# Twelve of sixteen gate channel tiles from half-depth block products, ahead of the attention heads

## The chip, the cores and the metric

The kernel runs on one core of a Trainium2 chip. The metric is the device time of one execution in microseconds. The profile's times count from the start of its own span, which is a little shorter than the device time of a run.

## What is computed

One layer of a block that joins a convolution branch and an attention branch, on 1024 tokens of 1024 channels, in float32. Cut to what matters here:

```python
h = rms_norm(x, norm1_g)
glu_in, q, k, v, gate_logits = split(h @ w_in)       # gate_logits: 2 x 1024 channels
a = glu(glu_in); a = depthwise_conv(a, conv_w) + conv_b
y_a = silu(rms_norm(a, conv_norm_g)) @ w_conv_out
o = dilated_window_attention(rms_norm(q), rms_norm(k), v)     # 16 heads of 64
y_b = o @ w_attn_out
g_a, g_b = split(sigmoid(gate_logits + gate_b))
x = x + (g_a * y_a + g_b * y_b) @ w_out
x = x + glu(conv3(rms_norm(x, norm2_g) @ w_up)) @ w_down
```

The change concerns `gate_logits`: 2048 gate channels by 1024 tokens, each a sum over 1024 channels of the normed x.

## The kernel before

Every float32 operand of a matrix product is split into a high part (a rounded copy, made on ScalarE) and a low part (the rest, a subtraction on VectorE), and each product is made of three TensorE matmuls: high x high, high x low, low x high (`split` L77, `gemm_half` L106). A plain gate tile of 128 channels by 512 tokens over the full depth of 1024 is thus 8 steps of 3 matmuls of 128x128 by 512.

The stages are, in order: norm1, its transposed high and low parts `hT`, and the GLU with first products (to about 181 us); the q, k, v products (loop at L607, to 457 us), with the convolution on VectorE and ScalarE beside them and a little beyond; the sixteen heads (to about 902 us); the merge with w_attn_out and w_out; the up projection, convolution of width 3 and the down projection, both of which already work by seven half-depth products instead of eight (`product` L971).

The gates and `w_conv_out` have no stage of their own. `side_steps` (L179) is a generator that gives out one step (three matmuls) at a time: 32 uses of gate weights (16 channel tiles, two token halves, L198 `gate`) and 16 of `w_conv_out` (L215 `conv_out`), 8 steps each, 384 in all. Per use it stages the weights by a 512 KB DMA, and asks for their splits as pieces of 128x512, which are handed out one by one (`piece_high` on ScalarE, `piece_low` on VectorE). The gate's sum leaves PSUM by a ScalarE activation that adds the bias (L210), and is stored to DRAM (`dgate`); the merge loads it again and takes the sigmoid (L834, L835).

Who asks for steps: `cover` (L641) takes 15, 8 and 20 steps around the end of the convolution branch and its norm (L650 to L676). Then the heads: 128 slots (16 heads, two halves of 512 queries, four blocks of 128 each). In each slot PE does the score of one block (`score`, two matmuls for each stretch of keys), the transposes of an earlier block (`flip`, BACK = 5 slots behind) and its product with v (`weigh`, L731 and L732); VectorE takes the masked minimum (L702), ScalarE the exponential (L707), GpSimd the division (L711); ScalarE and VectorE split the transposed block (L79, L80). Between these, `fill` (L749) takes steps from `side_steps`, by the rates in FILL, whose sum over eight slots is 17.5. What is left of the steps is done behind the last slot.

In the heads the program's order on ScalarE, VectorE and TensorE is kept as written (`tc.manual_schedule`); elsewhere a scheduler orders each engine's instructions at build. DMAs are issued by SyncE in one order (some by ScalarE); a DMA waits there for the one eight places ahead, and for what its data and its buffer need, and all behind it wait too. The loads of head 0 (`head(0)`, L625: six of 256 KB for q, kh, kl and one of 512 KB for the mask m) are issued before the gates begin, into a pool of their own (`p2i`), and those of head h + 1 in the third slot of head h.

Behind the heads, the merge (L825) takes, for each of eight output tiles and two halves, 24 matmuls `yb` of w_attn_out with the heads' output `oT`, which is loaded back from DRAM and split.

Of the kernel before, what the change touches and what calls it, by code (L numbers as in the profile page):

```python
# [13 lines left out]
F32 = mybir.dt.float32  # L14
# [21 lines left out]
FILL = (1.5, 3.4, 1.8, 1.9, 1.6, 3.0, 2.1, 2.2)  # L36
BACK = 5
SHARE = 0.6
COVER = (15, 8, 20)
# [14 lines left out]
def block_kernel(ctx: ExitStack, tc: tile.TileContext, x, xT, x0, g2, pack, mask,  # L54
# [76 lines left out]

    def spill(dst, src):
        sp.dma_start(dst.bitcast(F32), src.bitcast(F32))
# [7 lines left out]
    dv = [dr.tile([P, 8, 8, P], F32R, name=f"dv{i}") for i in range(2)]  # L141
    dgate = [dr.tile([P, T], F32, name=f"dgate{i}") for i in range(16)]
# [36 lines left out]
    def side_steps(hT, da):  # L179
# [18 lines left out]
        def gate(c, half):  # L198
            def go(w):
                gp = bank_ps(f"gate_{c}_{half}")  # L200
                if c >= 12 and half == 1:
                    if not aT:
                        aT.extend(hb_tiles(hb1, "aT"))
                    ask_conv(0, 2 * (c - 12))
# [5 lines left out]
                act.activation(sg, gp, AF.Identity, bias=pk[:, C_GB + c : C_GB + c + 1])  # L210
# [19 lines left out]
        for c in range(12):  # L230
            for half in range(2):
                gate(c, half)
        for half in range(2):
            for c in range(12, 16):
                gate(c, half)
        for c0 in (0, 4):
# [8 lines left out]
        for i, (_, n, go) in enumerate(uses):  # L245
# [7 lines left out]
            if n.startswith("co"):  # L253
                need = max(need, marks[(i - 32) // 4 % 2])
# [25 lines left out]
    with tc.tile_pool(name="ph1", bufs=1) as p1:  # L280
# [157 lines left out]
        with tc.manual_schedule(engines={ENG.Activation, ENG.DVE, ENG.PE}):  # L438
# [30 lines left out]
            for k in range(KT):  # L469
# [5 lines left out]
                low(1, k)  # L475
                if k == 6:
# [14 lines left out]
            for k in range(KT):  # L491
# [3 lines left out]
                settled1 = low(0, k)  # L495
        pair(1, 1, range(8), HH + HL + LH, 1)
# [124 lines left out]
        p2i_cm = tc.tile_pool(name="ph2i", bufs=1, side="right", reuse_waits="tile")  # L621
        p2i = p2i_cm.__enter__()

        def head(h):
            hp, r, g8 = h // 2, (h % 2) * DH, h // 8  # L625
            q = p2i.tile([P, T], F32R, tag="q", bufs=2, name=f"q_{h}")
            kh = p2i.tile([P, T], F32R, tag="kh", bufs=2, name=f"kh_{h}")
            kl = p2i.tile([P, T], F32R, tag="kl", bufs=2, name=f"kl_{h}")
            m = p2i.tile([P, T], F32, tag="m", bufs=2, name=f"m_{h}")
# [8 lines left out]
        gates = side_steps(hT, da)  # L638

        def cover(n):  # L640
            for _ in range(n):  # L641
                next(gates)
                one_piece()

        cover(COVER[0])
        with tc.issue_after(settled1.ins):
            conv_acc = conv_branch()


        pss = bank_ps("pss")  # L650
        for tt in range(8):
            summed = pe.matmul(pss[:, tt : tt + 1], sqacc[:, tt * P : (tt + 1) * P], ones[:, 0:1], start=True, stop=True)
        rs8 = p1.tile([P, 8], F32, name="crs8")
        cs8 = p1.tile([P, 8], F32, name="css8")
        rstd_of(rs8, pss[:, 0:8], D, cs8)
        with tc.issue_after(summed.ins):
            cover(COVER[1])
        dgs = p1.tile([P, CW - 1 + T], F32, tag="apad", bufs=10, name="dgs")[:, 0:T].rearrange("p (a b) -> p a b", a=8)
        dve.tensor_tensor(out=dgs, in0=ident.unsqueeze(1).to_broadcast([P, 8, P]),
                          in1=rs8.unsqueeze(2).to_broadcast([P, 8, P]), op=ALU.mult)  # L660
        for tt in range(8):
            if tt % 4 == 0:
                psr = bank_ps(f"psr_{tt}")
            spread2 = pe.matmul(psr[:, (tt % 4) * P : (tt % 4 + 1) * P], ones, dgs[:, tt, :], start=True, stop=True)
            if tt % 4 == 3:
                dve.tensor_copy(sqacc[:, (tt // 4) * 512 : (tt // 4) * 512 + 512], psr)
        for c in range(8):
            ct = conv_acc[c]
# [762 lines left out]
```

## Time and profile before

| what | value |
|---|---|
| median of 3 runs | 1744.92 us |
| lowest, highest | 1744.41, 1745.88 us |
| span of the profiled execution | 1741.8 us |
| granted TensorE clock | 1.00 in every window read |
| matmuls recorded | 8207 |
| end of the qkv loop, last head product | 457 us, 902 us |

A page of the profile gives busy times for PE (TensorE's matmuls), PEld (its weight loads), DVE (VectorE), ACT (ScalarE), POOL (GpSimd) and SP (SyncE, which issues DMAs). A row of a group reads: line, engine, operation, output <- input by the program's names, count, then busy us in all and mean ns of one, then idle time just ahead of them and what ended most of it. A row of a timeline reads: start us, duration us, engine, line, operation. A row of windows reads: busy us of the five engines, the granted clock, the DMA share and GB/s.

### The profile page before, as it was taken

Reading aid. Unit: us, or ns where it says so; the run is one execution under the profiler, and the core shown is the slowest. Engines: PE = TensorE matmul, PEld = TensorE weight load, DVE = VectorE, ACT = ScalarE, POOL = GpSimd, SP = SyncE. Lnnn points to the kernel's source line nnn. Section 1 sums busy time; section 2 is a strip of 40 time slices with the busy share of each in tenths; the row PEclk is TensorE's granted clock in tenths of the full one; section 3 lists DMA queues with packets and bytes.
Section 4 is the critical chain, followed back from the end, with each engine's and each line's share of the span. In section 5 each row is a group of like instructions: output and inputs, shape, how many; then the busy total and the mean of one; then the engine's idle time right before and its main releaser. Section 6 shows DMA issues by size and latency. Waiting matters only on the chain.

```text
span 1741.8 us, 22805 instructions
## 1 busy us (share of the span) xinstructions
PE 1737.4 (100%) x8207; PEld 1449.2 (83%) x8207; DVE 1301.5 (75%) x2005; ACT 797.1 (46%) x1276; POOL 174.5 (10%) x188
## 2 busy tenths in 40 slices
PE   9999999999999999999999999999999999999999
PEld 7888888888888888888888888888888888888887
DVE  5999999999756666677654573787777776889873
ACT  5421233323276666667663342555445544633431
POOL 0000232132012222222200000000000000000000
PEclk9999999999999999999999999999999999999999
DMA  7211145345686456657456576632222222398851
GB/s 295 73 54 50 53 135 170 109 140 175 174 274 180 148 159 168 179 161 225 128 179 210 178 271 236 218 121 73 97 80 77 85 85 85 127 362 310 295 176 49
DMA packets 149633, 276.99 MB, mean 159 GB/s; under 512 B 12048, under 2 KB 61840, under 8 KB 149520
## 3 DMA queue, kind: packets, MB, share of 16 engines
q1 hardware_dynamic: 147072, 269.11, 47.1%
q10 hardware_dynamic: 2448, 6.42, 0.9%
q8 instruction: 64, 1.05, 0.2%
q14 instruction: 49, 0.40, 0.1%
HBM read 202.09 MB, written 73.40 MB: 158 GB/s over the span
## 4 chain that ended last, share of the span: by engine, by line
PE 99%; DMA 0%; SPq 0%; DVE 0%; issue 0%; ACT 0%; DVEq 0%; ACTq 0%
PE dx L1243 7%; PE xz L976 6%; PE xz L975 6%; PE xz L977 6%; PE dy L1243 5%; PE qkv L130 5%; PE qkv L128 5%; PE qkv L129 5%; PE pp L717 4%; PE gate L111 3%; PE gate L112 3%; PE gate L113 3%; PE y L976 2%; PE y L977 2%; PE y L975 2%; PE o L732 2%
## 5 line engine op out<-in xcount | busy, mean ns | idle before, releaser
L80 DVE TENSOR_TENSOR pl<-pp,ph 128x512 fp32r<-128x512 f32 (+2 forms) x191 | 100.2, 553 | 90.1 <-ACT ph L79 90.0
L128 PE MATMUL qkv<-hi_qkv,hT 128*128 128x512 f32 x384 | 151.0, 394 | 0.0
L130 PE MATMUL qkv<-hi_qkv,hT 128*128 128x512 f32 x384 | 150.2, 392 | 0.0
L129 PE MATMUL qkv<-lo_qkv,hT 128*128 128x512 f32 x384 | 149.6, 391 | 0.0
L79 ACT ACTIVATE ph<-pp 128x512 fp32r<-128x512 f32 (+2 forms) x191 | 86.7, 489 | 115.9 <-PE pp L717 115.6
L702 DVE CUSTOM_DVE_ANT_0 p<-s,m 128x128 f32<-128x128 f32 (+3 forms) x120 | 90.5, 754 | 44.1 <-PE s L698 39.7
L711 POOL TENSOR_SCALAR p<-p,st 128x128 f32<-128x128 f32 (+3 forms) x120 | 90.3, 752 | 281.7 <-DVE st L710 222.4
L1146 DVE SCALAR_TENSOR_TENSOR u<-u,pk 128x1023 f32<-128x1023 f32 x88 | 112.3, 1278 | 1.2 <-ACT u L1144 0.9
L111 PE MATMUL gate<-hT,hi_gt 128*128 128x512 f32 x256 | 102.3, 400 | 0.0
L112 PE MATMUL gate<-hT,hi_gt 128*128 128x512 f32 x256 | 100.4, 392 | 0.0
L113 PE MATMUL gate<-hT,lo_gt 128*128 128x512 f32 x256 | 100.3, 393 | 0.0
L104 POOL TENSOR_TENSOR rs<-ss,mhalf 128x8 f32<-128x8 f32 x32 | 67.0, 2096 | 295.7 <-DVE ss L103 295.6
L707 ACT ACTIVATE p<-p,st 128x128 f32<-128x128 f32 (+3 forms) x120 | 93.0, 775 | 2.7 <-DVE st L702 2.0
L556 DVE SCALAR_TENSOR_TENSOR cacc<-csum,both,cacc 128x512 f32<-128x512 f32 x120 | 89.5, 746 | 1.2 <-ACT cacc L554 0.9
L556 DVE SCALAR_TENSOR_TENSOR cacc<-apad,pk,cacc 128x512 f32<-128x512 f32 x120 | 87.6, 745 | 0.0
L130 PEld LDWEIGHTS qkv<-hi_qkv,hT 128*128 128x128 f32 x384 | 72.1, 188 | 14.9
L129 PEld LDWEIGHTS qkv<-lo_qkv,hT 128*128 128x128 f32 x384 | 72.2, 188 | 14.4
L80 DVE TENSOR_TENSOR lo_uv<-raw_uv,hi_uv 128x1024 fp32r<-128x1024 f32 x20 | 24.5, 1226 | 79.7 <-ACT hi_uv L79 79.7
L128 PEld LDWEIGHTS qkv<-hi_qkv,hT 128*128 128x128 f32 x384 | 72.1, 188 | 14.1
L556 DVE SCALAR_TENSOR_TENSOR codd<-apad,pk,codd 128x513 f32<-128x513 f32 x112 | 83.7, 748 | 0.0
L717 PE MATMUL pp<-ident,p 128*128 128x128 f32 x540 | 78.9, 273 | 0.0
L717 PEld LDWEIGHTS pp<-ident,p 128*128 128x128 f32 x540 | 65.6, 140 | 14.9 <-DVE pl L80 0.5
(370 smaller groups left out, 4846.3 us busy)
## 6 DMA issues: line engine op xcount, KB each, us to landing
wr<-w_down SPq DMA_DIRECT2D x45, 512.0 KB, 5.8
gr<-dff SPq DMA_DIRECT2D x62, 256.0 KB, 5.1
raw_qkv<-w_qkv SPq DMA_DIRECT2D x24, 512.0 KB, 4.4
dff<-u SPq DMA_DIRECT2D x22, 512.0 KB, 2.6
raw_uv<-w_up SPq DMA_DIRECT2D x21, 512.0 KB, 3.2
raw_ug<-w_up SPq DMA_DIRECT2D x20, 512.0 KB, 3.2
dv<-v SPq DMA_DIRECT2D x16, 512.0 KB, 3.2
raw_gt<-w_ch SPq DMA_DIRECT2D x16, 512.0 KB, 3.8
```

The source lines that it names most:

```text
L111: pe.matmul(o, hi[:, k, :], ah[:, k, :], start=(k == 0), stop=False)
L112: pe.matmul(o, hi[:, k, :], al[:, k, :], start=False, stop=False)
L113: pe.matmul(o, lo[:, k, :], ah[:, k, :], start=False, stop=(k == KT - 1))
L128: pe.matmul(ps, ah, hi[:, k % 2, :], start=(k == 0), stop=False)
L129: pe.matmul(ps, ah, lo[:, k % 2, :], start=False, stop=False)
L130: pe.matmul(ps, al, hi[:, k % 2, :], start=False, stop=(k == KT - 1))
L556: dve.scalar_tensor_tensor(out=out_, in0=src[:, i : i + size], scalar=w(i), in1=out_, op0=ALU.mult, op1=ALU.add)
L717: pe.transpose(pp[:, qb * P : (qb + 1) * P], pts[qb][:, kt * P : (kt + 1) * P], ident)
L975: pe.matmul(o, wh[:, k, :], bh[:, k, :], start=(start and k == 0), stop=False, skip_group_check=not start)
L976: pe.matmul(o, wh[:, k, :], bl[:, k, :], start=False, stop=False, skip_group_check=not start)
L977: end = pe.matmul(o, wl[:, k, :], bh[:, k, :], start=False, stop=(k == 3), skip_group_check=not start)
L1243: pe.matmul(banks[n][:, cols], a[:, c], b[:, d], start=(start and i == 0 and m == 0), stop=(stop and i == nf - 1 and m == 2), skip_group_c ...
```

## The change

The gate tiles 0 to 11 form six pairs of 256 channels. For each, the 256 x 1024 block of weights and the 1024 x 1024 block of normed x are cut in 2 x 2 blocks of half the depth, and the four output quarters are formed from seven block products instead of eight (84 matmuls for each of six pairs, 504 in all). To this end:

- the normed x is also stored to DRAM (`dh`, 4 MB, eight DMAs of 512 KB during norm1) and read back after the convolution branch; VectorE forms four sums of its quarters, which are split (`token_forms`); one of the forms takes the place of the high and low parts of hT's half 1 at its first four depth tiles, which are first spilled (`db12`, two DMAs of 1 MB) and fetched again after the last pair;
- for each pair the weights' sums are formed (`gate_sums`; two extra loads of weights for the first two pairs), split, and used in `gate_first` (two products) and `gate_rest` (five products, with partial sums taken out by ScalarE copies and VectorE additions into quarter buffers, then stored);
- the conv branch's norm and its eight results run between the pairs (`conv_factors`, `conv_spread`, `conv_result`);
- tiles 12 and 13 (PLAIN) run as before, as cover ahead of all this; tiles 14 and 15 (LATE) and `w_conv_out` stay beside the heads, as 160 steps, with FILL rates whose sum is 8.1;
- the loads of head 0 come after the pairs in the program, and the pools of the heads are opened there;
- the bias of the gates moves to the sigmoids in the merge;
- the kernel is built with a DMA scratch size of 1024.

```diff
-FILL = (1.5, 3.4, 1.8, 1.9, 1.6, 3.0, 2.1, 2.2)
+FILL = (0.7, 1.55, 0.85, 0.9, 0.75, 1.4, 0.95, 1.0)
-COVER = (15, 8, 20)
+PLAIN = (12, 13)
+LATE = (14, 15)
+PAIRS = ((0, 1), (2, 3), (4, 5), (6, 7), (8, 9), (10, 11))
+COVER = 15
...
+    def product(o, wh, wl, bh, bl, start):
+        for k in range(4):
+            pe.matmul(o, wh[:, k, :], bh[:, k, :], start=(start and k == 0), stop=False, skip_group_check=not start)
+            pe.matmul(o, wh[:, k, :], bl[:, k, :], start=False, stop=False, skip_group_check=not start)
+            end = pe.matmul(o, wl[:, k, :], bh[:, k, :], start=False, stop=(k == 3), skip_group_check=not start)
+        return end
...
-                act.activation(sg, gp, AF.Identity, bias=pk[:, C_GB + c : C_GB + c + 1])
+                act.activation(sg, gp, AF.Copy)
...
+                if k % 2:
+                    sp.dma_start(dh[:, k - 1 : k + 1, 512:1024], xts[1][k // 2])
...
+        for i in range(2):
+            spill(db12[i], hT[i][1][:, 0:4, :])
+        early_gates = side_steps(hT, da, PLAIN, ())
...
+        def gate_first(c, w):
+            xz = big_ps(f"gx_{c}")
+            for i in range(2):
+                product(xz[:, i * 512 : i * 512 + 512], four(w[0])[:, 4 * i : 4 * i + 4], four(w[1])[:, 4 * i : 4 * i + 4],
+                        *left[i], True)
+            return xz
+
+        def gate_sums(c, v):
+            g = stage(w_ch[16 + c], f"gg{c}")
+            s = wp.tile([P, 1024], F32, tag="raw", bufs=4, name=f"gs12_{c}")
+            a11, a12, a21, a22 = v[:, 0:512], v[:, 512:], g[:, 0:512], g[:, 512:]
+            s1, s2 = s[:, 0:512], s[:, 512:]
+            tt(s1, a21, a22, add)
+            tt(s2, s1, a11, sub)
+            sw = wsplit(s, f"gs12_{c}")
+            tt(a21, a11, a21, sub)
+            gw = wsplit(g, f"gs3_{c}")
+            tt(a12, a12, s2, sub)
+            return [four(t) for t in sw], [four(t) for t in gw], a12
+
+        def gate_rest(c0, c1, xz, sw, gw, s4):
+            X, Z = xz[:, 0:512], xz[:, 512:1024]
+            Y = bank_ps(f"gy_{c0}")
+            c11 = quarter(f"gq11_{c0}")
+            act.activation(c11, X, AF.Copy)
+            dve.tensor_tensor(out=c11, in0=Z, in1=c11, op=add)
+            sp.dma_start(dgate[c0][:, t0], c11)
+            product(X, sh[:, 4:8], sl[:, 4:8], *form["t2"], False)
+            c12 = quarter(f"gq12_{c0}")
+            act.activation(c12, X, AF.Copy)
+            product(Y, sh[:, 0:4], sl[:, 0:4], *form["t1"], True)
+            p5 = quarter(f"gp5_{c0}")
+            act.activation(p5, Y, AF.Copy)
+            product(X, gh[:, 0:4], gl[:, 0:4], *b12, False)
+            c22 = quarter(f"gq22_{c0}")
+            dve.tensor_tensor(out=c22, in0=X, in1=p5, op=add)
+            sp.dma_start(dgate[c1][:, t1], c22)
+            s4h, s4l = [four(t) for t in wsplit(s4, f"gs4_{c0}")]
+            product(Y, s4h, s4l, *b22, False)
+            dve.tensor_tensor(out=c12, in0=Y, in1=c12, op=add)
+            sp.dma_start(dgate[c0][:, t1], c12)
+            product(X, gh[:, 4:8], gl[:, 4:8], *form["t4"], False)
+            c21 = quarter(f"gq21_{c0}")
+            act.activation(c21, X, AF.Copy)
+            sp.dma_start(dgate[c1][:, t0], c21)
+
+        def token_forms(i):
+            r22, r12, r11, r21 = (load(n, k, half) for n, k, half in (("22", 4, 1), ("12", 0, 1), ("11", 0, 0), ("21", 4, 0)))
+            tt(r22, r22, r12, sub)
+            tt(r12, r12, r11, sub)
+            tt(r11, r22, r11, add)
+            for dst, src in ((form["t2"], r11), (form["t1"], r12), (b12, r22)):
+                if src is r22:
+                    tt(r21, r21, r11, sub)
+                split(dst[0][:, ks], dst[1][:, ks], view(src))
+            split(form["t4"][0][:, ks], form["t4"][1][:, ks], view(r21))
...
+        nexts = [(gate_first(a, w),) for (a, _), w in zip(PAIRS, first)]
+        nexts[0] += again(0)
+        for n, (a, b) in enumerate(PAIRS):
+            gate_rest(a, b, *nexts.pop(0))
+            if not n:
+                nexts[0] += again(1)
+            if n == 0:
+                rs8 = conv_factors()
+            elif n == 1:
+                conv_spread(rs8)
+            elif n < 4:
+                for c in range(4 * (n - 2), 4 * (n - 1)):
+                    conv_result(c)
+            if n + 2 < len(PAIRS):
+                v, w = gate_weights(PAIRS[n + 2][0])
+                nexts.append((gate_first(PAIRS[n + 2][0], w),) + gate_sums(PAIRS[n + 2][1], v))
+        for i in range(2):
+            fetch(b12[i], db12[i])
...
         tiles = {0: head(0)}
...
+        gates = side_steps(hT, da, (), LATE)
...
-                act.activation(ga, ga, AF.Sigmoid)
-                act.activation(gb, gb, AF.Sigmoid)
+                act.activation(ga, ga, AF.Sigmoid, bias=pk[:, C_GB + c : C_GB + c + 1])
+                act.activation(gb, gb, AF.Sigmoid, bias=pk[:, C_GB + 8 + c : C_GB + 9 + c])
```

## Prediction on record, made before any run of the changed kernel

> **What bounds the kernel now.** I read the page first: engine totals, slices, chain. Then the groups of the instructions that change.
>
> ```profile
> span 1741.8 us, 22805 instructions
> PE 1737.4 (100%) x8207; PEld 1449.2 (83%) x8207; DVE 1301.5 (75%) x2005; ACT 797.1 (46%) x1276; POOL 174.5 (10%) x188
> ...
> PEclk9999999999999999999999999999999999999999
> ...
> PE 99%; DMA 0%; SPq 0%; DVE 0%; issue 0%; ACT 0%; DVEq 0%; ACTq 0%
> ...
> L111 PE MATMUL gate<-hT,hi_gt 128*128 128x512 f32 x256 | 102.3, 400 | 0.0
> L112 PE MATMUL gate<-hT,hi_gt 128*128 128x512 f32 x256 | 100.4, 392 | 0.0
> L113 PE MATMUL gate<-hT,lo_gt 128*128 128x512 f32 x256 | 100.3, 393 | 0.0
> ```
>
> TensorE works from end to end at full clock; the chain is PE for 99%; the 768 gate matmuls never waited (last column). So a matmul less is a gain at its price, and any new stall of PE is a loss in full. The price is the distance of two starts, not the mean duration of 0.39 us, since matmuls overlap. The timeline of PE at the end of the qkv loop:
>
> ```profile
> 457.07 0.39 PE L130 MATMUL qkv<-hi_qkv,hT 128*128 128x512 f32 x1
> 457.30 0.39 PE L111 MATMUL gate<-hT,hi_gt 128*128 128x512 f32 x1
> 457.53 0.39 PE L112 MATMUL gate<-hT,hi_gt 128*128 128x512 f32 x1
> 457.75 0.39 PE L111 MATMUL gate<-hT,hi_gt 128*128 128x512 f32 x1
> ```
>
> That is (457.75 − 457.07) / 3 = 0.227 us. Windows by stage (columns: PE, PEld, DVE, ACT, POOL busy, clock, DMA share, GB/s), first in the heads, then behind them:
>
> ```profile
> 600.00:650.00 50.00, 50.00 (x278) 42.60 (x277) 30.94 (x80) 30.35 (x69) 12.26 (x17) 1.00 0.56 158
> 900.00:950.00 50.00, 50.00 (x224) 41.46 (x223) 24.09 (x27) 22.37 (x30) 0.00 (x0) 1.00 0.61 206
> ```
>
> In the heads DVE and ACT have a third of their time free. What covers their latency is the filler: gate and conv_out matmuls between the heads' own. The change takes filler away, so its cost is decided at the places where PE then has nothing to issue.
>
> **The change part by part.**
>
> *Matmuls.* Before, the twelve tiles of the pairs are 12 × 2 halves × 24 = 576 matmuls. After, 6 pairs × 7 products × 12 = 504. The 72 saved are worth 72 × 0.227 = **−16.3 us**. Everything else must be held against this.
>
> *Forming tokens and weights.* DVE gets 8 sums and 8 splits of 128x1024 for the token forms, and per pair four sums of 512, three wide splits, a narrow one and three adds out of PSUM. The nearest rows are these, from the groups and from the timelines of DVE and ACT:
>
> ```profile
> L80 DVE TENSOR_TENSOR lo_qkv<-raw_qkv,hi_qkv 128x1024 fp32r<-128x1024 f32 x24 | 29.2, 1219 | 0.9 <-ACT hi_qkv L79 0.9
> 466.64 0.68 DVE L567 TENSOR_TENSOR sqacc<-sqacc,codd 128x512 f32<-128x512 f32 x1
> 483.90 3.49 DVE L669 TENSOR_TENSOR cacc<-cacc,sqacc 128x1024 f32<-128x1024 f32 x3
> 901.02 0.60 ACT L225 ACTIVATE ya<-ya 128x512 f32<-128x512 f32 x1 [1.94 <-PE ya L113]
> ```
>
> Per pair DVE needs 3 × 1.22 + 8 × 0.68 = 9.1 us beside 84 × 0.227 = 19.0 us of matmuls: hidden, and the eight conv results (1.16 each) with it. The token forms take 8 × (3.49/3 + 1.22) = 19.1 us, and mostly follow the conv branch, which ends at 467.3. That gives about 486; the weight sums of the first pair and their split (0.68 × 2 + 1.22, ACT's half ahead) lead to 489.5. PE reaches the first product that needs these after two plain tiles (96 matmuls) and two first halves (48): 457.3 + 144 × 0.227 = 490.0. A near tie: I take **+1**, between 0 (scheduler starts forms earlier) and 4 (one more wide sum and split in front).
>
> *Accumulators in the pairs.* The first products of pair n+2 go into the PSUM buffer that pair n has just left, whose last use is ACT's copy. Nothing, or two matmuls, stands between: end of the matmul 0.39 − 0.23, wake-up 0.1 (in the tail's rows below hi_ao ends at 913.23 and lo_ao starts at 913.26; I round up), copy 0.60, wake-up 0.1, so 0.95 us with nothing between and 0.5 with two. Four such turns and one copy between back-to-back products of the last pair: **+3.3**. Bounds 0 and 8 (ACT held up by a 1.1 us split each time).
>
> *The handover to the heads* is the largest term. Before, head 0's loads were issued while gates ran, 20 us ahead of use; SP's timeline:
>
> ```profile
> 466.20 0.51 SPq L136 DMA_DIRECT2D q<-dq  x1
> 466.81 0.55 SPq L136 DMA_DIRECT2D kh<-dk  x1
> 467.41 0.59 SPq L136 DMA_DIRECT2D kl<-dk  x1
> 468.05 0.59 SPq L136 DMA_DIRECT2D q<-dq  x1
> 468.68 0.59 SPq L136 DMA_DIRECT2D kh<-dk  x1
> 469.32 0.59 SPq L136 DMA_DIRECT2D kl<-dk  x1
> 469.95 1.66 SPq L634 DMA_DIRECT2D m<-mask  x1
> ```
>
> And the DMA issues (KB each, median us from issue to landing):
>
> ```profile
> q<-dq SPq DMA_DIRECT2D x32, 256.0 KB, 5.4
> kl<-dk SPq DMA_DIRECT2D x32, 256.0 KB, 6.6
> m<-mask SPq DMA_DIRECT2D x16, 512.0 KB, 7.6
> v<-dv SPq DMA_DIRECT2D x16, 512.0 KB, 3.5
> dgate<-gs SPq DMA_DIRECT2D x32, 256.0 KB, 3.9
> gg<-dgate SPq DMA_DIRECT2D x32, 256.0 KB, 3.5
> ```
>
> In the changed order of SP, which issues in turn, these seven stand behind the store of the last pair's c21 quarter. That store waits for ACT's copy, and the copy for the pair's last product. Queued with them ahead are the two 1 MB refetches of hT, v of two heads and the other quarters. PE has nothing between that product and the first score: the plain tile 14 stands behind scores 0 and 1. So PE waits 0.16 + 0.1 + 0.60 for the copy, some 0.5 for the store's issue, 469.32 − 466.20 = 3.1 for the issues up to the last kl (all six land before a score can run), and 6.6 to its landing: **11**. From below, 3.5 instead of 6.6 (the fastest row of a 256 KB load): 8. From above, seven landings crowded by refetches: 14. Then the first softmax needs m, which is issued 0.6 later, takes a 1.7 us issue, and lands 7.6 after: 1.6 later than kl. Behind that come DVE's minimum, ACT's exponential and the reciprocal, and only then on DVE the low half of tile 14's weights, which PE's filler needs. The rows for the first three:
>
> ```profile
> 490.62 0.29 DVE L702 CUSTOM_DVE_ANT_0 p_first<-s,m 128x128 f32<-128x128 f32 x1 [3.23 <-PE s L698]
> 494.58 1.28 ACT L707 ACT_TABLE_LOAD   x1
> 495.87 0.40 ACT L707 ACTIVATE p_first<-p_first,st_first 128x128 f32<-128x128 f32 x1
> ```
>
> 1.6 + 0.29 + 0.40 + 0.1 + 0.68 and four wake-ups of 0.1 make 3.5; less 0.9 of scores, 2.6, and 1.28 more if the table load is late. I take **+3**, so the handover is **+14**, between 8 and 18.
>
> The trace never shows PE at rest, so it cannot say what the granted clock does after 11 us of it. The Trainium skill, TensorE: Matmul & The Clock Gate, Part 1: The HAM clock gate, says that an idle window of about 3.4 us lowers the clock to half, until as long a stretch of work. By it the sum would be some 2 to 4 us higher; the row for the clock (9 in every slice) neither supports nor refutes it.
>
> *Heads with half the filler.* The FILL sums are 17.5 and 8.1 for eight slots, so 1.175 steps of three matmuls less per slot: 0.80 us. A slot took (901.5 − 490.6) / 133 = 3.09 us (starts of the first softmax above and of the last o below), now 2.29. DVE has 30.94/50 × 3.09 = 1.91 per slot and ACT 1.88. PE stays the bound by 0.4 on average, but slots with eight transposes have a chain through ACT and DVE of about their own length. **+2**, from 0 to 13 (0.1 for each slot).
>
> *Tail.* Behind the last o, 117 conv_out matmuls stood as cover; now 8 steps, 24 matmuls, 5.4 us. What the first yb needs, as it ran before:
>
> ```profile
> 901.50 0.28 PE L731 MATMUL o<-ph,v 128*128 128x256 f32 x1
> ...
> 901.79 0.28 PE L732 MATMUL o<-pl,v 128*128 128x128 f32 x1
> ...
> 902.11 0.59 ACT L742 ACTIVATE ot<-o 64x512 f32<-64x512 f32 x1 [0.49 <-PE o L732]
> 903.27 0.62 ACT L835 ACTIVATE gg<-gg 128x512 f32<-128x512 f32 x1
> 905.53 3.90 ACT L79 ACTIVATE oT<-raw_o 128x1024 fp32r<-128x1024 f32 x4 [0.61 <-DVE gg L836]
> 907.88 1.47 SPq L84 DMA_DIRECT2D raw_ao<-w_ao  x2
> 912.17 1.06 ACT L79 ACTIVATE hi_ao<-raw_ao 128x1024 fp32r<-128x1024 f32 x1 [2.11 <-PE ya L112]
> 913.26 1.23 DVE L80 TENSOR_TENSOR lo_ao<-raw_ao,hi_ao 128x1024 fp32r<-128x1024 f32 x1 [2.00 <-ACT hi_ao L79]
> ...
> 928.51 0.39 PE L111 MATMUL yb<-oT,hi_ao 128*128 128x512 f32 x1
> ```
>
> lo_ao was ready 14 us ahead. In the changed order ACT has ot 0.59, four oT highs 3.90, a ya copy 0.60, the table load 1.28, sigmoids 1.24 and hi_ao 1.06: about 9.3 behind the last o, and lo_ao 1.2 later. PE runs dry at 5.4: 3.9 until the first matmul of yb, about 0.8 at the third, which needs lo_ao. **+5**; 0 if the next stage's loads come sooner, 9 if raw_ao, issued behind an oT low, lands late.
>
> *Early stores* (dh, 4 MB, eight DMAs, and 2 MB of spill): SP gets 8 more issues ahead of weights. PE never waited for weights in qkv; cost **0**, at most 3 if those weights come late.
>
> Sum: −16.3 + 1 + 3.3 + 14 + 2 + 5 = **+9.0**. Against the profiled execution's 1741.8 that is 1750.8; the median of the runs shown, 1744.92, lies 3.1 above the span, so **1754 us**.
>
> **The rivals.**
>
> *Stalls at their lower ends (faster).* Deciding point: new idle of PE below 16.3. With the handover at 8 (loads land in 3.5, table load early), pairs at 1.5, heads and tail near 1 each, it is 11.5, so −4.8: 1740. With the tail and pairs free too, 1737 down to 1734. For it: DMA is at 0.56 in the heads, so 256 KB can land faster than the medians. Against it: six loads in one queue behind a store that waits for the very last product.
>
> *Heads bound by the chain DVE–ACT–PE.* At 0.1 us for each of 128 slots, 13 in place of 2: 1765. For it: 1.91 against 2.29, with uneven slots; against it: BACK leaves five slots between score and transposes.
>
> *Clock falls after the gap.* A stretch as long as the handover's shorter part, or a slot (3 us), at half speed costs its own length again. Two gaps long enough, handover and tail: 1.5 to 3 each, 1754 + 4 = 1758. The Trainium skill's page named above states the mechanism; no row here bears it out, so it gets a small chance.
>
> *The pairs save nothing*: if the half-depth products were split or repeated, PE would show over 504 matmuls for them. Then 1754 + 16 = 1770. The loops count out to 504, so 2 in 100.
>
> **How the numbers follow.** Forecast, with its parts between 17 and 33 (1745 to 1762): 0.50. Stalls at lower ends (1730 to 1745): 0.26. Heads bound: 0.14. Clock: 0.08. No saving: 0.02. The range is 1738 to 1768: it leaves out about the lower third of the faster rival (0.1) and the far ends above (0.1). 0.2%, 3.5 us, is about what a measurement of this kernel can tell from no change: below 1741.4 lies 0.20 (most of the faster rival), from there to 1748.4 0.14, above 0.66. Signs are mixed, but the forecast's own range, 1745 to 1762, is nearly all on the slower side.
>
> **What would show it.** Right: 72 matmuls fewer in the first part; an idle PE of 8 to 14 us at the first score, released by kl or q; a second one of some 3 us ahead of tile 14's first steps, released by DVE; some 4 to 5 us ahead of the first yb, released by hi_ao and lo_ao; half a microsecond to one at the firsts of pairs 2 to 5, released by ACT copies; windows in the heads with PE at 49 to 50 of 50. Wrong: a first score that starts within 5 us of the last product, heads' windows below 48 (the chain rival), PEclk below 9 in the slice after the handover (the clock rival), idle in qkv for weights (early stores).

## The result and the profile after

The changed kernel takes 1787.89 us (median of 4 runs, 1787.64 to 1789.52) against 1744.66 for the kernel before: slower by 2.5%, ratio 1.025 (95% interval 1.0235 to 1.0264). The forecast was 1754, range 1738 to 1768: the sign was right, the size far too small. The page of the changed kernel, the lines that answer to those shown of before:

```profile
span 1787.7 us, 22813 instructions
PE 1740.9 (97%) x8135; PEld 1439.9 (81%) x8135; DVE 1348.2 (75%) x2063; ACT 815.0 (46%) x1284; POOL 174.4 (10%) x188
...
PEclk9999999999999899999999999999999999999999
...
PE 89%; DMA 4%; DVE 2%; ACT 2%; issue 2%; POOL 1%; SPq 0%; ACTq 0%; DVEq 0%; POOLq 0%
```

There are 72 matmuls fewer (8207 − 8135), as the loops say. But PE is no longer the whole chain, and one slice shows a clock below full. Who PE waited for, longest in total first (columns: total us, times, longest); before, this list was empty but for 1.0 us at the start:

```profile
PE s L836 <- DMA kh<-dk: 13.6, 1, 13.6
PE yb L114 <- ACT hi_ao L82: 6.5, 3, 5.1
PE pp L856 <- POOL p L850: 5.5, 10, 0.7
PE gate L114 <- ACT hi_gt L186: 3.9, 1, 3.9
PE o L871 <- DVE pl L83: 2.1, 4, 1.1
PE gx L138 <- DVE gq L710: 1.9, 1, 1.9
PE gy L138 <- ACT hi_gs L82: 1.8, 2, 0.9
```

Most of these waits stand where the forecast put them (that for POOL is its rival's), and the seven sum to 35 us; but a span longer by 45.9 with 16.3 us of work less means 62 us lost. The rest must be pauses too short for this list, or a slower clock. I therefore laid both timelines of PE side by side and took the distance of starts in excess of the work (0.227 us for 512 columns, in proportion for fewer), stage by stage.

**Handover.** PE of the changed kernel around the last pair product, then SP:

```profile
606.96 0.39 PE L140 MATMUL gx<-gt,lo_gs 128*128 128x512 f32 x1
620.97 0.45 PE L836 MATMUL s<-kh,q 128*128 128x128 f32 x1 [13.62 <-DMA kh<-dk]
622.19 0.45 PE L837 MATMUL s<-kl,q 128*128 128x128 f32 x1 [0.77 <-DMA kl<-dk]
...
627.07 0.80 PE L114 MATMUL gate<-hT,hi_gt 128*128 128x512 f32 x1 [3.90 <-ACT hi_gt L186]
627.66 0.63 PE L115 MATMUL gate<-hT,hi_gt 128*128 128x512 f32 x1
628.09 0.63 PE L116 MATMUL gate<-hT,lo_gt 128*128 128x512 f32 x1
628.51 0.63 PE L114 MATMUL gate<-hT,hi_gt 128*128 128x512 f32 x1
```

```profile
605.75 1.35 SPq L149 DMA_DIRECT2D v<-dv  x2
608.05 0.32 SPq L729 DMA_DIRECT2D dgate<-gq  x1
608.47 0.51 SPq L149 DMA_DIRECT2D q<-dq  x1
609.04 0.59 SPq L149 DMA_DIRECT2D kh<-dk  x1
610.13 0.45 SPq L149 DMA_DIRECT2D kl<-dk  x1
...
612.73 0.45 SPq L149 DMA_DIRECT2D kl<-dk  x1
614.02 0.33 SPq L812 DMA_DIRECT2D m<-mask  x1
```

The queue stands as forecast: the store of c21 (608.05), then head 0's loads. But the loads, issued over 3.1 us before, now take 4.3 (608.47 to 612.73), because four of the six wait for an earlier transfer to land, and they land 7.6 to 9.3 us behind their issue, the last kl 9.3, against the 6.6 of the forecast: the refetches and v are under way. From the last product to tile 14's first step 19.9 us pass, 19.5 of them without work (forecast 14). What ends the last wait is ACT, which loads a table behind the first minimum and makes the high half of tile 14's weights behind the first exponential:

```profile
624.70 1.28 ACT L846 ACT_TABLE_LOAD   x1 [16.67 <-DVE st L841]
...
626.40 1.13 ACT L186 ACTIVATE hi_gt<-raw_gt 128x512 fp32r<-128x512 f32 x2
```

And then the gates run at half speed: 0.42 us from start to start (628.09 to 628.51). The windows give the granted clock (the number behind POOL's count), here with the other two places where it falls:

```profile
594.00:597.00 3.00, 3.00 (x10) 2.41 (x10) 0.00 (x0) 0.00 (x0) 0.00 (x0) 0.67 0.27 104
627.00:630.00 3.00, 2.94 (x7) 2.32 (x8) 1.29 (x2) 1.02 (x4) 0.16 (x1) 0.50 1.04 218
633.00:636.00 3.00, 2.77 (x16) 2.17 (x15) 2.97 (x9) 2.29 (x6) 1.77 (x2) 1.00 0.03 12
970.00:973.00 3.00, 2.42 (x5) 1.51 (x6) 1.61 (x2) 2.16 (x3) 0.00 (x0) 0.58 1.04 408
```

The three stretches cost 1.1, 2.5 and 1.9 us (excess of starts), 5.5 together.

**Heads.** Their pace is read from the first minimum of a head (the one of 128x128), eight heads apart; DVE's timeline of before, then of after:

```profile
632.78 0.29 DVE L702 CUSTOM_DVE_ANT_0 p<-s,m 128x128 f32<-128x128 f32 x1 [0.41 <-PE pp L717]
...
831.26 0.29 DVE L702 CUSTOM_DVE_ANT_0 p<-s,m 128x128 f32<-128x128 f32 x1 [0.42 <-DMA kh<-dk]
```

```profile
722.62 0.28 DVE L841 CUSTOM_DVE_ANT_0 p<-s,m 128x128 f32<-128x128 f32 x1
...
879.61 0.28 DVE L841 CUSTOM_DVE_ANT_0 p<-s,m 128x128 f32<-128x128 f32 x1
```

A head took 24.81 us, now 19.62. The filler taken away is 9.4 steps of 3 matmuls, 6.4 us; so each head loses 1.2 us, 19 to 21 over sixteen. Less than half of it is in the list of waits. The windows:

```profile
700.00:750.00 50.00, 49.06 (x276) 40.38 (x275) 40.98 (x108) 39.21 (x90) 15.82 (x21) 1.00 0.83 222
850.00:900.00 50.00, 48.09 (x276) 40.86 (x275) 37.73 (x101) 36.10 (x80) 15.08 (x20) 1.00 0.64 171
```

A PE busy for 48 to 49 of 50 looks nearly full; what this hides is seen from start to start. Once per head the last block's transposes wait for POOL's division (PE's timeline of after):

```profile
880.91 0.49 PE L856 MATMUL pp<-ident,p 128*128 128x128 f32 x3
882.08 0.77 PE L856 MATMUL pp<-ident,p 128*128 128x128 f32 x5 [0.68 <-POOL p L850]
```

From start to start that is 0.8 us per head in the mean of eight heads; the rest is 0.3 from the transposes to the product with v (1.28 to 1.56 per head in excess of the work, that wait apart) and 0.2 between the high and the low product (0.76 to 0.95), each below 0.1 us a time.

**Tail.** The first yb came 5.3 us late, two later waits for hi_ao lost 1.9 more, and the clock 1.9:

```profile
965.04 0.39 PE L116 MATMUL ya<-aT,lo_co 128*128 128x512 f32 x1
970.54 0.79 PE L114 MATMUL yb<-oT,hi_ao 128*128 128x512 f32 x1 [5.12 <-ACT hi_ao L82]
```

From the first matmul of w_out on, the two profiles stand 45.9 us apart and stay so.

### The profile page after: what moved, and what is told of

It reads as the page before. It is cut to its first block, busy times and chain, and to the rows that moved or that the text cites. A ratio compares the mean times of both kernels' runs of the same rounds, so it can differ in the third digit from the quotient of the medians.

```text
span 1787.7 us, 22813 instructions
## 1 busy us (share of the span) xinstructions
PE 1740.9 (97%) x8135; PEld 1439.9 (81%) x8135; DVE 1348.2 (75%) x2063; ACT 815.0 (46%) x1284; POOL 174.4 (10%) x188
## 3 DMA queue, kind: packets, MB, share of 16 engines
q8 instruction: 64, 1.05, 0.2%
## 4 chain that ended last, share of the span: by engine, by line
PE 89%; DMA 4%; DVE 2%; ACT 2%; issue 2%; POOL 1%; SPq 0%; ACTq 0%; DVEq 0%; POOLq 0%
PE dx L1369 7%; PE xz L138 6%; PE xz L140 6%; PE xz L139 6%; PE dy L1369 5%; PE qkv L131 5%; PE qkv L133 5%; PE qkv L132 5%; PE pp L856 3%; PE y L138 2%; PE y L140 2%; PE y L139 2%; PE o L870 2%; PE o L871 2%; PE wo L133 2%; PE wo L132 2%
## 5 line engine op out<-in xcount | busy, mean ns | idle before, releaser
L846 ACT ACTIVATE p<-p,st 128x128 f32<-128x128 f32 (+3 forms) x120 | 93.0, 775 | 12.8 <-DVE st L841 11.0
L856 PE MATMUL pp<-ident,p 128*128 128x128 f32 x540 | 83.4, 276 | 5.9 <-POOL p L850 5.5
L83 DVE TENSOR_TENSOR lo_uv<-raw_uv,hi_uv 128x1024 fp32r<-128x1024 f32 x20 | 24.5, 1225 | 79.8 <-ACT hi_uv L82 79.8
L836 PE MATMUL s<-kh,q 128*128 128x128 f32 (+2 forms) x192 | 66.0, 344 | 13.6 <-DMA kh<-dk 13.6
L870 PE MATMUL o<-ph,v 128*128 128x512 f32 (+2 forms) x191 | 74.5, 394 | 0.6
L138 PE MATMUL xz<-h2left,hi_uv 128*128 128x512 f32 x176 | 68.6, 390 | 0.0
```

Source lines behind the costliest of these rows:

```text
L83: dve.tensor_tensor(out=lo, in0=src, in1=hi.bitcast(F32), op=ALU.subtract)
L138: pe.matmul(o, wh[:, k, :], bh[:, k, :], start=(start and k == 0), stop=False, skip_group_check=not start)
L856: pe.transpose(pp[:, qb * P : (qb + 1) * P], pts[qb][:, kt * P : (kt + 1) * P], ident)
L870: pe.matmul(o[:, c], v[:, kt, :], ph[:, c], start=(kt == 0), stop=False)
```

## The experiments

The theory: four things cost time, each for itself. (1) Head 0's loads stand behind the pairs' stores and refetches on SP. (2) With half the filler a head is held by the chain score, minimum, exponential, reciprocal, division, transposes. (3) The cover behind the last o is too short. (4) The clock falls after gaps. Rivals: the heads lose by the change's own traffic or by fixed costs; the handover is bandwidth, whatever the order. Times are medians; before, on the same chips, took 1743.8 to 1744.4.

### e_loads: head 0's loads first

```diff
+            st = act if c0 == PAIRS[-1][0] else sp
...
-            sp.dma_start(dgate[c1][:, t1], c22)
+            st.dma_start(dgate[c1][:, t1], c22)
...
-        for i in range(2):
-            fetch(b12[i], db12[i])
...
         tiles = {0: head(0)}
+        behind_head = head_last[0]
+        with tc.issue_after(behind_head.ins):
+            for i in range(2):
+                fetch(b12[i], db12[i])
...
-        values(0)
+        with tc.issue_after(behind_head.ins):
+            values(0)
```

The stores of c12 and c21 change in the same way; `head_last[0]` is the last load of head 0, its m.

> The changed kernel, with head 0's seven loads issued ahead of the two 1 MB refetches and of v, and the last pair's last three quarters stored through ACT's queue, so that no store stands ahead of the loads. Theory (the 13.8 us gap ahead of the first score, the wait for m behind it and the slow clock that follows are all due to the place of these loads in SP's order): the first score starts within 2 us of the last pair product, tile 14's first step 2 to 4 us later, the clock stays at 1.00, and the time falls by 15 to 21 us, to 1767 to 1773. Rival (the transfers are slow in themselves, or the first softmax chain takes the place of the wait): the first filler step still comes more than 8 us after the last product, and the time falls by 5 to 9, to about 1780.

1775.09 us, 12.8 less than the changed kernel. The first score follows the last product at once (607.54), but tile 14's first step comes at 614.23, and the clock falls again. PE and SP of this run:

```profile
607.54 0.22 PE L840 MATMUL s<-kh,q 128*128 128x128 f32 x1
608.70 0.33 PE L841 MATMUL s<-kl,q 128*128 128x128 f32 x1 [0.94 <-DMA kl<-dk]
...
614.23 0.79 PE L114 MATMUL gate<-hT,hi_gt 128*128 128x512 f32 x1 [4.92 <-ACT hi_gt L186]
```

```profile
596.97 0.59 SPq L149 DMA_DIRECT2D kh<-dk  x1
605.09 0.44 SPq L149 DMA_DIRECT2D kl<-dk  x1
609.30 0.34 SPq L811 DMA_DIRECT2D m<-mask  x1
```

It lies between the two forecasts. The last kl and m were held for 8 and 4 us: the order in which a DMA waits for the one eight places ahead runs over both queues, so that SP waited for the stores which I had moved to ACT (these landed at 605.08 and 609.28; kl was issued at 605.09, m at 609.30).

### e_lead: the stores on POOL's queue, 8 filler steps ahead of the heads

```diff
+            st = pool if c0 == PAIRS[-1][0] else sp
...
         gates = side_steps(hT, da, (), LATE)
+        for _ in range(8):
+            next(gates)
+            one_piece()
```

with FILL (0.65, 1.45, 0.8, 0.85, 0.7, 1.3, 0.9, 0.95) and the rest as in e_loads; the loads of aT are queued behind head 0's.

> As e_loads, but the last pair's last three quarters are stored through POOL's queue, and 8 filler steps of tile 14 are taken ahead of the heads (FILL 7.6), so that its weights are split before the first softmax. In e_loads kl was issued at 605.1 and m at 609.3, and tile 14's first step still came 6.7 us behind the last product. Theory (what is left of the handover is this late m, and the split of tile 14's weights behind the first softmax on ACT and DVE): PE waits under 1.5 us in all between the last pair product and the fourth score, the clock stays at 1.00 there, and the time falls by 7 to 10 us below e_loads, to 1765 to 1768. Rival (the first slots are a chain of score, softmax and division that nothing covers): the wait moves behind the first scores, and the gain over e_loads is under 4.

1775.95 us, against 1765 to 1768 by the theory. The handover is nearly gone: SP issues all seven loads from 593.43 to 597.18, the first score starts at 609.36 and a filler step at 610.59, and the mean clock is 0.998 (0.992 in the changed kernel). The scheduler put the 8 steps into the pair stage. Yet nothing was gained over e_loads. That is the rival's number, but not its reason: behind the first scores one wait of 2.0 us is left, and the loss is in later heads. Heads 4 to 7 now take 20.2 to 21.4 us instead of 19.4 to 19.8, with waits for POOL of 8.5 us in all, and each head has some 1.5 filler matmuls less. What was saved ahead was lost in heads that have no slack, so handover and heads do not simply add up here.

### b_halffill: the kernel before, with the changed kernel's filler

```diff
-FILL = (1.5, 3.4, 1.8, 1.9, 1.6, 3.0, 2.1, 2.2)
+FILL = (0.7, 1.55, 0.85, 0.9, 0.75, 1.4, 0.95, 1.0)
```

> The kernel before, with nothing changed but FILL, which takes the changed kernel's numbers (sum 8.1 in place of 17.5): no pairs, all sixteen gate tiles plain; about half of the steps move from the heads to behind the last o, where nothing hinders them. Theory (heads with 24 filler matmuls each instead of 52 lose 1.2 to 1.4 us each, whatever stands ahead of them): 1762 to 1767, and head lengths near 19.6 us. Rival (the heads' loss comes from what the change adds, its loads and pools beside the heads): 1745 to 1750.

1767.17 us, 23.0 more than before, with not one matmul or transfer added or left out. Its heads, and its wait for POOL:

```profile
585.94 0.28 DVE L702 CUSTOM_DVE_ANT_0 p<-s,m 128x128 f32<-128x128 f32 x1
...
742.60 0.28 DVE L702 CUSTOM_DVE_ANT_0 p<-s,m 128x128 f32<-128x128 f32 x1
```

```profile
PE pp L717 <- POOL p L711: 7.0, 11, 1.1
```

(742.60 − 585.94) / 8 = 19.58 us a head, the changed kernel's 19.62. From the second head on the pace costs some 19 us; about 5 more are lost in the first slots, where one score waits for 3.2 us and the clock is at half for 3.4 us (497.75 to 501.16). The heads alone so outweigh the 16.3 us that the pairs save, and their loss comes from the filler taken away, not from what the change adds.

### b_half_nodiv and b_half_back6: what holds these heads

In b_half_nodiv POOL's division of the softmax is left out; b_half_back6 has the transposes a slot later.

```diff
-            pool.tensor_scalar(pt, pt, st[:, 2:3], 1.0, op0=ALU.mult, op1=ALU.mult)
```

```diff
-BACK = 5
+BACK = 6
```

> b_halffill with POOL's division of the softmax left out, so that the transposes take the exponentials as they are (the output is not divided by the softmax's sum). If the heads' loss is the chain minimum, exponential, reciprocal, division in two slots, it goes with one of its four parts: heads of 18.3 to 18.9 us instead of 19.6, no wait of transposes for POOL, 1750 to 1757. If the loss is VectorE's own load or the fixed cost of changing between transposes and wide matmuls, the heads stay above 19.3 and the time above 1762.

> b_halffill with BACK 6: the transposes one slot later, so that the same chain has three slots. Chain theory: as in b_half_nodiv, heads of 18.6 to 19.2 us, 1752 to 1760. In e_back6 only heads 7 to 12 gained (18.7 against 19.6) and others lost some; if that is due to the order and not to the pairs, the gain here is about 5 us again.

b_half_nodiv: 1757.81 us, 9.4 less than b_halffill. Its heads:

```profile
582.79 0.28 DVE L702 CUSTOM_DVE_ANT_0 p<-s,m 128x128 f32<-128x128 f32 x1
...
733.62 0.28 DVE L702 CUSTOM_DVE_ANT_0 p<-s,m 128x128 f32<-128x128 f32 x1
```

18.85 us, and no wait for POOL is left in its list (the longest that remains for transposes is 0.2 us, for DVE's pl). The time is 0.8 us above its forecast. One might think that GpSimd's work had slowed VectorE down. But VectorE's rows are as long without it (its minimum of 128x1024 takes 1225 ns, against 1224 in b_halffill), but for the low halves of the side steps' weights, one a head (0.68 us against 0.89); these take 0.68 in the changed kernel too, and its heads are as long as b_halffill's. So the division in the chain is about 0.7 of the 1.2 us per head; 0.5 stay. b_half_back6: 1761.83 us, 5.3 less and 1.8 above the 1752 to 1760 of its forecast; the waits for POOL are gone there too, most heads take 18.8 to 19.3, but heads 4, 14 and 15 take 20.3 to 20.5. That the division's place in the chain costs time is shown twice; for the remaining half a microsecond I have only the excess between transposes and products, not a cause.

### e_back6, e_fillpos, e_tail: the same heads in the changed kernel

e_back6 is BACK = 6. The other two change FILL:

```diff
-FILL = (0.7, 1.55, 0.85, 0.9, 0.75, 1.4, 0.95, 1.0)
+FILL = (0.5, 3.0, 0.7, 0.7, 0.5, 1.2, 0.75, 0.75)     # e_fillpos
+FILL = (0.5, 1.2, 0.65, 0.7, 0.55, 1.1, 0.75, 0.75)   # e_tail
```

> The changed kernel with BACK 6 in place of 5: the transposes come one slot later behind the scores. Theory (with slots of 2.45 us in place of 3.1 the chain score, minimum, exponential, division on POOL is longer than the two slots between the last score of a half and its transposes, and PE waits there once per head): the waits of the transposes for POOL vanish, 0.8 us for each of 16 heads, 10 to 14 us in all, to 1774 to 1778. Rival (the heads' excess is the fixed cost of changing between short transposes and wide matmuls, which nothing covers any more): no change beyond 3 us.

> The changed kernel with the same sum of FILL, 8.1, but 3.0 of it in the slot whose transposes wait for POOL (0.5, 3.0, 0.7, 0.7, 0.5, 1.2, 0.75, 0.75). Theory of the POOL chain: one more filler step of 0.68 us stands ahead of these transposes, so the wait of 0.5 to 0.7 per head shrinks to near nothing, 6 to 11 us in all, unless other slots are laid bare in turn. Rival (fixed costs of changing): same time within 3 us.

> The changed kernel with FILL summing to 6.2 instead of 8.1: 31 steps (21 us of matmuls) move from the heads to behind the last o. If PE is still the bound in the heads, they shorten by all of 21 us, the stall ahead of the first yb and its slow clock (9 us together) go, and the time falls by 7 to 9, to about 1780. If the heads are held by the chain through DVE, ACT and POOL, they shorten by 8 to 15 only, and the time stays or rises: 1785 to 1795.

e_back6: 1783.55, 4.3 less, under half of the 10 to 14 of the chain theory: the waits for POOL are gone and heads 7 to 12 take 18.5 to 18.9 us, but the others from the second on 19.2 to 20.5, and the first yb waits for 7.1 us instead of 5.1. e_fillpos: 1787.45, no gain, which is the rival's number; but the waits for POOL are gone but for 0.5 us, as the chain theory has it. Heads 11 to 14 have almost no idle PE, but other slots, robbed of filler, wait instead: the wait for DVE's pl rises from 2.1 to 5.1 us in all. Filler is short in more than one slot. e_tail: 1791.66, 3.8 more, as the chain theory has it. With 5.7 filler matmuls less (1.3 us) a head is only 0.4 us shorter: of the 21 us of matmuls moved behind the last o some 13 are lost, against the 9 that the tail gives back.

### e_ao: w_attn_out staged ahead of o

```diff
+        ao_raw = [stage(w_ao[c], f"ao{c}") for c in range(2)]
         load_split(oT, do_, 0, "o")
-        ao_raw = [stage(w_ao[c], f"ao{c}") for c in range(2)]
```

> The changed kernel with one line moved: the first two tiles of w_attn_out are staged ahead of the reload of o, so that their loads and splits come during the heads. Theory (the first yb waits for hi_ao, whose load stands behind o's splits): the stall of 5.1 us and its slow clock go or halve, 3 to 8 us less, 1780 to 1785. Rival (the chain o, store, reload, split of oT is as long): the stall stays, now for oT, and the time is the same within 2 us.

1788.27 us: the rival's time, but not its wait. The first yb starts 5.4 us behind the last o instead of 10.6, and no wait for oT takes the place; a wait of 6.3 us for the hi_ao of a later tile follows within yb. In e_tail, with 31 steps more behind the last o, no such wait is left: the tail lacks cover, and this other order did not replace it.

### e_pairs3, e_best3, e_best4: fewer pairs

e_pairs3 has three pairs, and tiles 6 to 11 plain beside the heads:

```diff
-PAIRS = ((0, 1), (2, 3), (4, 5), (6, 7), (8, 9), (10, 11))
+PAIRS = ((0, 1), (2, 3), (4, 5))
+MORE = (6, 7, 8, 9, 10, 11)
...
+FILL = (1.2, 2.7, 1.45, 1.5, 1.3, 2.4, 1.7, 1.75)
...
+        gates = side_steps(hT, da, MORE, LATE)
```

e_best3 adds e_lead's edits and FILL (1.05, 2.35, 1.25, 1.3, 1.1, 2.1, 1.45, 1.5); e_best4 is the same with four pairs and FILL (0.95, 2.05, 1.1, 1.15, 1.0, 1.85, 1.3, 1.35).

> Three pairs instead of six: tiles 0 to 5 from half-depth products, 6 to 11 plain beside the heads, FILL 14.0. The matmuls saved fall to 36, worth 8.2 us. If the heads' loss goes with the filler taken away (42 matmuls per head in place of 24), it falls from 20 to about 5, the pairs' own stalls from 9 to 5, and the handover (22) and the tail (9) stay: 1774 to 1780, better than six pairs. If the heads' loss is a fixed cost of the new order, the time rises by 5 to 8, to about 1794.

> Three pairs, with head 0's loads early and 8 filler steps ahead of the heads as in e_lead, and FILL 12.1, so that about 30 steps stay as cover behind the last o. In e_pairs3 the heads took 22.35 us with 42 filler matmuls each, no more than the kernel before at the same filler (12.83 beside the filler). Theory (only the filler per head, the place of head 0's loads and the cover behind the last o cost anything, and the saved matmuls are otherwise gained in full): -8.2 for 36 matmuls, +4 stalls in the pairs, +2 handover, +1 heads with 36 each, +1 tail: 1742 to 1747. Rival (there are further losses in the new order): above 1752.

> The same with four pairs, two plain tiles in halves more for the pairs, FILL 10.75 (32 filler matmuls per head). -10.9 for 48 matmuls, +4, +2, +1 as in e_best3; the heads are near the point where the chain through DVE and POOL takes over: their PE time would be 12.85 + 32 x 0.227 = 20.1 us against the 19.3 to 20 us that heads with 24 took. Theory: +2 to +5 there, 1743 to 1748. If the chain already binds earlier: 1750 to 1756.

e_pairs3: 1769.93, 18 less than six pairs, though half the saving is given up, and 4 below its forecast. With 42 filler matmuls a head typically takes 22.35 us, 12.83 beside its filler, as before the change: the heads' loss sets in somewhere between 42 and 24. e_best3 (1767.78) and e_best4 (1769.87) lie over 20 us above the forecasts of their theory. The first yb no longer waits in e_best3, but the handover was back, by another way. SP of e_best3:

```profile
543.80 7.75 SPq L88 DMA_DIRECT2D raw_gt<-w_ch  x2
551.65 0.51 SPq L150 DMA_DIRECT2D q<-dq  x1
```

Two prefetches of gate weights wait there for DVE to free their buffers, and q stands behind them; the last pair product is at 551.6, and PE waits for 9.9 us.

### e_best3b, e_best4b, e_best4b_back6, e_best6b: these prefetches behind head 0

```diff
-            raw = stage(src, name)
+            with tc.issue_after(behind_head[0].ins) if behind_head and len(got) >= 3 else ExitStack():
+                raw = stage(src, name)
```

> e_best3, with the prefetches of gate weights beyond the first three tiles queued on SP behind head 0's loads. Ledger closes: the gap of 10 us ahead of the first score, the waits behind it (9 us, with hT's refetch) and the slow clock (2) go but for some 3 us, and the time falls by 16 to 19 us, to 1749 to 1752; left over are the pairs' stalls with one slow-clock stretch (9) and the heads (5) against 8.2 saved. Rival (another wait takes the place): above 1758.

> e_best4 with the same. Ledger closes: 15 to 18 us less, 1752 to 1755, for the heads lost some 10 us at 32 filler matmuls each (13.7 beside the filler instead of 12.85) against 2.7 more saved. Rival: above 1760.

> e_best4b with BACK 6. If the heads' loss at 32 filler matmuls is still the chain through POOL, as at 24 (where BACK 6 gave 4 to 5 us), 3 to 5 us less than e_best4b, near 1749. If at 32 it is the load of VectorE and ScalarE in some slots: within 2 us of e_best4b.

> e_lead with the same for its prefetches. In e_lead the handover was already 2 us and the loads early, so nothing changes beyond 3 us: 1773 to 1778, all of it the heads with 23 filler matmuls and the tail.

Three of the four differ from the kernels that they are held against in more than these prefetches, which their forecasts do not name:

```diff
-BACK = 5
+BACK = 6                       # e_best4b, e_best4b_back6 and e_best6b
...
-FILL = (0.65, 1.45, 0.8, 0.85, 0.7, 1.3, 0.9, 0.95)     # e_lead
+FILL = (0.7, 1.55, 0.85, 0.9, 0.75, 1.4, 0.95, 1.0)     # e_best6b
```

e_best4b and e_best4b_back6 are so one and the same program, and e_best4b's forecast was for the prefetches alone.

e_best3b: 1752.25, 0.25 above the range of its ledger. The score follows the last product without a gap; 2.8 us stay ahead of the gates, for hT's refetch. e_best4b: 1752.64, in its range, but in part by luck, for BACK 6 is in it too. e_best4b_back6: 1754.08, a second measurement of e_best4b; it says nothing on BACK. What BACK is worth at 32 filler matmuls is better seen against e_best4, which has BACK 5 and this wait:

```profile
PE pp L872 <- POOL p L866: 4.4, 9, 0.8
```

In e_best4b it is gone, and its heads, from the second on, take 20.6 us in the mean instead of 21.0 (13.3 beside the filler instead of 13.7). So the division probably still holds the heads at 32, though no run there changes BACK alone. e_best6b: 1771.32, 4.6 below e_lead and 1.7 below its forecast. With BACK 6 the 8.5 us of waits for POOL are gone, and the first yb now waits for 10.1 us; what the prefetches alone did cannot be told from it.

The best version, e_best3b, is still slower than the kernel before, by 0.46% (ratio 1.0046, interval 1.0033 to 1.0058): 36 matmuls, 8.2 us, do not pay for some 6 in the heads (13.3 beside the filler instead of 12.9), 5 at the handover with a slow stretch behind it, and 3 between the pairs' products; 2 more I have not traced. Its heads still wait 2.8 us in all for POOL; with BACK 6 it was not run.

## Why the prediction was wrong in size

| step | forecast | measured in the changed kernel |
|---|---|---|
| 72 matmuls saved | −16.3 | −16.3 (count of 8207 to 8135) |
| token forms, first t2 product | +1 | +1.4 |
| stalls between pair products | +3.3 | +6.8, and 1.1 of slow clock |
| handover | +14 | +19.5, and 2.5 of slow clock |
| heads with half the filler | +2 | +19 to 21, and some 1.4 in the first head |
| tail | +5 | +7.2, and 1.9 of slow clock |
| early stores | 0 | +0.6 |
| sum | +9.0 | +45 to 47 (profiles: +45.9) |

- **Heads**: this step failed, and it is half of the miss. I took the mean busy time of DVE and ACT per slot (1.91 and 1.88) against PE's 2.29 and called PE the bound. That asks whether an engine has time, not how long the way through all of them is. Against the rival I held that BACK leaves five slots between score and transposes. That is so for the first block of a half; its transposes need the fourth block too, and from the score of that one there are two slots. They shrank from 6.2 us to about 4.9, and the last block of a head needs 1.22 + 1.15 + 1.12 on DVE, ACT and POOL besides the score, the reciprocal and the waits in their queues. The rival named the chain and priced it at 13; b_halffill shows some 19 for the pace of the heads, and b_half_nodiv that the division's place in the chain is about half of it. The cause of the other half stays open. The condition was known from the rows; its chance, 0.14, was too low.
- **Handover**: the mechanism was right up to m (store of c21, six loads, then m), and the loads were mis-sized: 6.6 us of landing is the median of 32 loads, but in the same trace head 0's own last kl took 7.8; issued behind 3 MB of refetches and v it needed 9.3, and four of the six issues waited. The first score came 13.8 us behind the last product instead of 11. The last link was another: tile 14's first step waited for the high half of its weights on ACT, behind a table load of 1.28 us that I had counted only if late, and not for the low half on DVE; 5.6 us instead of 3. With 19.5 the term passed its upper bound of 18.
- **Clock**: a rival in the text, at 4 us and 0.08; it happened three times, 5.5 us in all, on top of the forecast case and not in place of it. The Trainium skill (TensorE: Matmul & The Clock Gate, Part 1: The HAM clock gate) says that the clock falls to half after an idle window of about 3.4 us. By that rule two stretches were due, and with gaps of 11 and 4 to 5 us in the forecast they belonged in its sum; half speed agrees (0.42 us against 0.227, a window at 0.50), the third stretch does not, for the longest gap ahead of it was 1.9 us, and shorter ones went ahead of such stretches in other runs (last section).
- **Pairs**: the two waits I named were there (0.7 each), but gy waited twice as well, 0.9 each, with ACT's hi_gs named as what released it, and the last pair 1.9 for a sum on DVE. Twice the forecast, within its bounds of 0 to 8.
- **Tail**: 5.3 for the first tile, much as worked out, though the six times given for ACT add up to 8.7, not 9.3; hi_ao was ready 10.6 us behind the last o, two waits for DMAs of 0.5 included. I had stopped there, and the weights of a later tile came late too.
- The range left out the sum of several terms at their upper ends. Each term was bounded from both sides, but 1745 to 1762 treated them as if their errors would cancel. All at their upper ends give 4 + 8 + 18 + 13 + 9 + 3 − 16.3 = 38.7, near 1784, and with the clock's 4 near 1788, where the kernel came out. They all went one way; a likely reason, not shown, is that each came from a trace without gaps.

## What to carry to other kernels

Filler beside a latency chain is not spare work: before moving it elsewhere, compare the length of the chain through all engines with the slots that it has, not each engine's busy time with the slot. Cutting the filler of the kernel as it is, in one line, measures the price before anything is built. And where a stage ends, look at what stands ahead of the next stage's loads on the queue that issues them, prefetches included; here the same gap had three different causes in turn (the pairs' stores and refetches, stores on another queue, prefetched weights).

## What the runs showed of the hardware that I had not expected

The granted clock fell to half for 3.41 us or a multiple of it (by the trace's record of the clock, in the changed kernel from 595.04 for 3.41, from 612.11 for 20.48 and from 970.51 for 3.41), and the gap ahead can be short. Ahead of the first of these it was 1.9 us (591.85 to 593.75), and the stretch began 1.3 us after work had resumed; in e_best3 it was 1.8 us, and the stretch began some 3 us after it. In e_fillpos it was 1.13 us (PE's timeline and a window of this run, then a window of e_best3; the granted clock stands behind POOL's count):

```profile
680.89 0.39 PE L871 MATMUL o<-pl,v 128*128 128x256 f32 x1 [1.13 <-DVE pl L83]
...
681.14:684.55 3.41, 3.41 (x12) 2.72 (x12) 0.87 (x5) 1.61 (x6) 2.05 (x3) 0.50 1.01 227
```

```profile
494.00:498.00 4.00, 4.00 (x14) 3.19 (x14) 2.27 (x5) 0.13 (x1) 0.00 (x0) 0.57 0.72 244
```

In e_loads (from 492.94) and e_tail (from 493.36) the longest gap just ahead was 0.88 and 0.67 us. On the other hand the same wait of 1.9 us was followed by no slow stretch in e_tail (594.12), nor was one of 2.0 us in e_lead. So the length of the gap alone does not decide; what does is not shown. And DMAs issued by ACT hold up those of SP eight places later, as e_loads showed.
